# Encoder block in float32: sum transfers paused in the branches, first row block ahead, branch sums on VectorE, temporaries in a pool of their own

## The chip, the cores and the metric

One core of a Trainium2 chip runs the whole program in one launch. The metric is device time in microseconds, from runs of the whole kernel; lower is better. The profile is of one execution on the same core. Engines are named as the profile names them: PE (TensorE), DVE (VectorE), ACT (ScalarE), POOL (GpSimd), SP (SyncE, which only issues transfers here).

## The reference

The input x has 2048 rows of 1024 float32 numbers. One layer is computed, followed by a last RMSNorm:

```
xn = rmsnorm(x);  z = xn @ w_in            # columns: pool | q | forget | input | output gate | branch gates
ya = pool_mixer(z_pool) @ w_pa             # 4 window means minus token, a 128x128 matrix per group
yb = hgrn2(q, forget, input, gate) @ w_pb  # gated linear recurrence, 4 heads of 128
x  = x + (sig(g0) * ya + sig(g1) * yb) @ w_o
h  = rmsnorm(x) @ w_up;  h = conv3(h) + b  # causal, per column
x  = x + (silu(gate half) * value half) @ w_down
return rmsnorm(x)
```

## The kernel before, in words

**Two halves.** The 2048 rows are done in two halves of 1024, and each half is two row blocks of 512 (`hf` 0 and 1). A half runs through the stages io, proj, pa, pb, wo (function `mixer`), then up and dn (`ffn`).

**Products.** Every float32 operand is cut in two parts of the type fp32r, high and low (`split`, L595 to L598: a cast on ACT or POOL, a subtraction on DVE), and a product is three matmuls: high by high, high by low, low by high. A product of a 128x512 operand over four k is 12 matmuls. The large matrix products (io, proj, wo, up, dn) use a Strassen-like scheme with seven products P1 to P7 in place of eight. It needs sums of quarters of the weights (`s1` to `s4`) and of the activations.

**Weights.** `Stream` loads weight tiles on SP's queue into 8 raw buffers (L182), cuts them in two into 6 operand buffers (L205 a cast on ACT, L206 a subtraction on DVE), and hands them out in program order. In the first half the sums of weight quarters for wo, up and dn are made in DRAM by transfers alone, in groups of up to four units (`Sums.make`: copies on ACT's queue, L278, and accumulating transfers on POOL's queue, L275). Each step of a group is a transfer of up to 1 MB. The task `prepare` takes two groups at a time and makes one step every 7 ticks; a tick is counted every 6 matmuls issued through `mm`. In the second half nothing of this runs: the sums are read again.

**The branches.** `pa` multiplies the pooled, mixed rows (`mx`, read back from DRAM by `pa_task` on SP's queue, L796, and split) by w_pa; `pb` does the same for the recurrence's output (`oT`, fetched by the task that `start_o` starts at the loop's step `O_AT`). Each goes over eight column tiles m in the order `M_ORDER` = 0, 4, 1, 5, 2, 6, 3, 7; for each m it makes one product for row block 0 and one for row block 1. The result is multiplied by a gate that is fetched from DRAM (`gl`, L1291 and L1293 on DVE). In pb the two branches are then added on POOL (L1301), and for each k = m - 4 the sums of the scheme are made from four of these tiles (`add_forms`, `yf`, L1090 on POOL).

**The row products.** `Rows` computes wo and dn: the activations' tiles (128x128 blocks of them) are the stationary operand and the weights move. `make(upto)` splits the operands of the steps up to a number; `run(p)` calls it LEAD = 5 steps ahead. At the end of a product, DVE adds PSUM banks to the rows (L1066).

**The up stage.** A `Unit` makes the seven products of one pair of column tiles into three PSUM banks X, Z and V, and takes temporaries e1, u2, u3 (`tmp`, L1018 to L1024). Near the end of up, `EARLY` makes the first operands of dn, whose rows `g_P` are fetched from DRAM on POOL's queue (L796).

**Room.** Most tiles come from one pool, `slots`, of 77 tiles of 128x528 float32. A tile is given out when a former one is released. Instructions are written in program order; the framework plans the order on each engine with a simulated timeline, and adds the waits.

Of the kernel before, what the change touches and what calls it, by code (L numbers as in the profile page):

```python
# [29 lines left out]
TB = 512  # L30
# [16 lines left out]
OUT = R_OUT, R_OUT_BANK, R_OUT_NEW, R_OUT_ADD  # L47
# [7 lines left out]
PROJ = (("fq", 0), ("g", 0), ("u", 0), ("fq", 1), ("g", 1), ("g", 2), ("fq", 2), ("g", 3),  # L55
        ("u", 1), ("g", 4), ("fq", 3), ("g", 5), ("g", 6), ("g", 7))

M_ORDER = (0, 4, 1, 5, 2, 6, 3, 7)

N_SLOTS = 77  # L60
N_RUN = 3
N_HEADS = 2
GO_AT = 5
# [1 line left out]
X_AT, X_AT2 = 1, 4  # L65
GO_IO = (("P2", 1), ("P2", 0))
G_POOL = 4
O_AT, O_LAG = 4, 1
FIN_WAIT = 4
N_RAW = 8  # L70
GROUP = 4
# [7 lines left out]
def tile_trunk(  # L79
# [15 lines left out]
    nc = tc.nc  # L95
    pe, act, dve, pool, sp = nc.tensor, nc.scalar, nc.vector, nc.gpsimd, nc.sync
# [3 lines left out]
    rawp = ctx.enter_context(tc.tile_pool(name="rawp", bufs=N_RAW))  # L100
    opsp = ctx.enter_context(tc.tile_pool(name="opsp", bufs=N_OPS))
    slots = ctx.enter_context(tc.tile_pool(name="slots", bufs=N_SLOTS))
    dram = ctx.enter_context(tc.tile_pool(name="dram", bufs=1, space=bass.MemoryType.DRAM))
    banks = ctx.enter_context(tc.tile_pool(name="banks", bufs=8, space=bass.MemoryType.PSUM))

    def slot(name, cols=TB, dt=F32):
        return slots.tile([P, cols], dt, tag="s", name=name, padded_shape=[P, 528])

    def bank(name, cols=512):
        return banks.tile([P, cols], F32, tag="b", name=name, padded_shape=[P, 512])  # L110
# [33 lines left out]
    def mm(*args, **kw):  # L144
        count[1] = pe.matmul(*args, **kw)  # L145
        count[0] += 1
        if count[0] % MM_PER_TICK == 0:
            tick()
# [102 lines left out]
    stream = Stream()  # L251
# [210 lines left out]
        return grouped(w_up_t, ms, [MF + m for m in ms], list(range(m0, m0 + n)))  # L462

    prep = []

    def prepare():
        todo = [sums[name].make(g) for name in ("wo", "up", "dn")
                for g in range(len(sums[name].groups))]
        active = []
        while todo or active:  # L470
            while todo and len(active) < 2:
                active.append(todo.pop(0))
            g = active.pop(0)
# [320 lines left out]
    def fetch(d, name, eng=sp):  # L794
        t = slot(name)
        eng.dma_start(t, d)  # L796
        return t
# [188 lines left out]
    class Unit:  # L986
# [3 lines left out]
            self.t = {}  # L990

        def tmp(self, k):
            t = slot(f"{self.name}_{k}")
            self.t[k] = t
            return t

# [87 lines left out]
    def add_forms(two, forms, k, name, store=lambda p, t: None, sums=True, pin=lambda i: None):  # L1084

        def comb(p, x0, x1, op):
            if (p, k) in forms or x0 is None or x1 is None:
                return
            t = slot(f"{name}_{p}_{k}")
            pin(pool.tensor_tensor(t, x0, x1, op))  # L1090
# [12 lines left out]
        comb("P3", forms.get(("P6", k)), two.get((1, 1)), ALU.add)  # L1103
# [54 lines left out]
    def mixer(b0, forms, late):  # L1158
# [103 lines left out]
        for n, (kind, i) in enumerate(PROJ):  # L1262
            if (kind, i) == ("u", 0):
                held["w"] = stream.get("pw")
            u = Unit(f"{kind[0]}r{b0}_{i}", "in", emits[kind](i))
            for p in ORDER:
                u.multiply(p, forms, late)
                u.after(p)
                if n == len(PROJ) - 1 and p == "P1":
                    mtask = Task(pa_task())  # L1270

        def branch(key, s, xs, evac, each):
            for n, m in enumerate(M_ORDER):
                each(n)
                for m2 in M_ORDER[n : n + 3]:
                    for hf in range(2):
                        gate(s, m2, hf)
                w4 = stream.get(key)
                for hf in range(2):
                    ps = bank(f"{key}{b0 + hf}_{m}")  # L1280
                    chain_t(ps, lambda k: (w4[:, 0, k * P : (k + 1) * P],
                                           w4[:, 1, k * P : (k + 1) * P]),
                            [xs[hf, k] for k in range(4)])
                    evac(m, hf, gate(s, m, hf), ps)
                stream.used(1)

        y, yf = {}, {}

# [9 lines left out]

        def evac_b(m, hf, g, ps):
            gated(g, hf, g, ps)  # L1300
            pool.tensor_tensor(y[m, hf], y[m, hf], g, ALU.add)  # L1301
# [17 lines left out]
        join(otask[0])  # L1319

        acc = {}

        def load_res(n):
            hf, j = n // NT, n % NT
# [27 lines left out]
    def ffn(b0, forms, late):  # L1352
# [74 lines left out]
        acc = {}  # L1427
        fg = []
        fss = {}
# [6 lines left out]
        def square(hf, j, c):  # L1436
            if (hf, j) not in fss:
                fss[hf, j] = small.tile([P, 4], F32, tag="fss", name=f"fss{b0}_{hf}_{j}")
            act.activation(slot(f"fj{b0}_{hf}_{j}_{c}"), acc[hf, j, c], AF.Square,  # L1439
                           accum_out=fss[hf, j][:, c : c + 1])  # L1440

        def final(hf, j):
            if hf == 1 and not last:
                yield FIN_WAIT
            for c in range(2):
                square(hf, j, c)
            halves = [acc.pop((hf, j, c)) for c in range(2)]
            res = [slot(f"fo{b0}_{hf}_{j}_{c}") for c in range(2)]
            ss = fss[hf, j]
            pool.tensor_tensor(ss[:, 2:3], ss[:, 0:1], ss[:, 1:2], ALU.add)  # L1450
            r = rstd_of(ss[:, 2:3], 1, 1.0 / D, f"f{b0}_{hf}_{j}r")
            yield 3
            rr = (b0 + hf) * TB + j * P
            for c in (1 - hf, hf):
                if (hf, c) == (0, 1):
                    act.activation(res[c], halves[c], AF.Copy, scale=r[:, 0:1])
                    pool.tensor_tensor(res[c], res[c], fg[c], ALU.mult)
                else:
                    dve.scalar_tensor_tensor(res[c], halves[c], r[:, 0:1], fg[c],  # L1459
                                             ALU.mult, ALU.mult)  # L1460
                sp.dma_start(out[rr : rr + P, 512 * c : 512 * c + 512], res[c])

        down = Rows(f"dn{b0}", "dn", DOWN, MF // 2,
                    lambda p, k: fetch(gd[p, k], f"g{b0}_{p}_{k}", pool), acc, 5)
        EARLY = {"P7": 2, "P4": 3}
        units = {}
        for n, (m, p) in enumerate(up_order()):
            if n == GO_AT:
# [7 lines left out]
            drain(1)  # L1476
            if m == MF - 1 and p in EARLY:
                down.make(EARLY[p])

# [61 lines left out]


# [46 lines left out]
```

## Time and profile before

| what | value |
|---|---|
| median of 3 runs | 2625.63 us (2621.32 to 2626.07) |
| profiled execution, first to last instruction (span) | 2614.3 us |
| PE busy in it | 2533.7 us, 97% |
| DVE, ACT, POOL busy | 1967.4, 1168.9, 909.3 us |
| mean granted PE clock | 0.989 |
| HBM read, written | 384.94 MB, 187.17 MB |

The profiled execution's device time is not given apart from its span; the span is 7.0 us below the fastest of the three runs and 11.3 us below their median. Stages are recognised by the tile that PE writes: `io_`, `fr_`/`ur_`/`gr_` (proj), `pa`, `pb`, `wo_P`, `up_`, `dn_P`. In a timeline row stand the start in us, the duration in us, engine, line, operation, output and inputs, shapes and count, and in brackets the idle time of the engine before it and what ended that. An SP row is a transfer being issued.

### The profile page before, as it was taken

How to read it: one execution, taken by the hardware profiler on the slowest of the kernel's cores; microseconds unless marked ns; L12 is line 12 of the kernel's file. 1: busy time of each engine (PE TensorE's matmuls, PEld its weight loads, DVE VectorE, ACT ScalarE, POOL GpSimd, SP SyncE). 2: the span in 40 equal slices, each digit the busy share in tenths (PEclk: the TensorE clock that was granted, in tenths of full speed). 3: DMA queues.
4: the chain of work that ended last, by engine and by line, in shares of the span. 5: the costliest groups of instructions: out<-in, count | busy, mean ns of one | idle time of the engine just before them, and what ended most of it. 6: DMA issues, size and time to landing. Idle time of an engine off the chain costs nothing. (4 is left out here: it accounts for less than half of the span.)

```text
span 2614.3 us, 35569 instructions
## 1 busy us (share of the span) xinstructions
PE 2533.7 (97%) x11464; PEld 2064.8 (79%) x11464; DVE 1967.4 (75%) x3390; ACT 1168.9 (45%) x2204; POOL 909.3 (35%) x1253
## 2 busy tenths in 40 slices
PE   7899999989999999999999999999999999999998
PEld 6788888767778888878878788887787888887887
DVE  7898779358799877876476787774778987787845
ACT  5333434224555544555364344442345554445633
POOL 5544343062444343362141111200623433335402
PEclk9999999999999999999999999999999999999999
DMA  6887868888778897587365344346452445545943
GB/s 221 274 213 211 224 189 242 268 275 214 198 188 241 243 240 198 165 305 255 108 195 157 101 135 121 116 145 218 142 173 84 151 150 148 141 141 185 377 142 105
DMA packets 254059, 496.90 MB, mean 190 GB/s; under 512 B 26736, under 2 KB 43248, under 8 KB 253552
## 3 DMA queue, kind: packets, MB, share of 16 engines
q1 hardware_dynamic: 187968, 319.89, 38.9%
q0 software_dynamic: 41504, 110.64, 16.6%
q10 hardware_dynamic: 24400, 64.08, 7.1%
q8 instruction: 91, 1.49, 0.2%
q14 instruction: 96, 0.79, 0.1%
HBM read 384.94 MB, written 187.17 MB: 219 GB/s over the span
## 5 line engine op out<-in xcount | busy, mean ns | idle before, releaser
L205 ACT CAST ops<-raw 128x512 fp32r<-128x512 f32 x732 | 451.6, 620 | 780.1 <-PE dn_P L145 141.1
L206 DVE TENSOR_TENSOR ops<-raw,ops 128x512 fp32r<-128x512 f32 x732 | 564.1, 775 | 214.2 <-ACT ops L205 208.7
L1381 DVE SCALAR_TENSOR_TENSOR e<-h,cols,e 128x512 f32<-128x512 f32 x176 | 142.4, 813 | 29.9 <-ACT e L1379 26.1
L1379 ACT ACTIVATE e<-h,cols 128x512 f32<-128x512 f32 x176 | 142.6, 814 | 24.2 <-DVE h L984 16.9
L1384 DVE SCALAR_TENSOR_TENSOR e<-h,cols,e 128x512 f32<-128x512 f32 x176 | 133.9, 769 | 3.0
L796 POOL DMA_DIRECT2D g_P<-dg_P x154 | 83.7, 545 | 107.6 <-PE dn_P L145 70.0
L1090 POOL TENSOR_TENSOR gf_P<-e,e 128x512 f32<-128x512 f32 x44 | 67.8, 1542 | 153.1 <-DVE e L1390 97.8
L1090 POOL TENSOR_TENSOR gf_P<-gf_P,e 128x512 f32<-128x512 f32 x44 | 60.1, 1366 | 68.5 <-DVE e L1390 68.1
L1374 POOL COPY h<-h 128x2 f32<-128x2 f32 x88 | 40.7, 482 | 113.9 <-DVE h L982 112.0
L1301 POOL TENSOR_TENSOR ya<-ya,gl 128x512 f32<-128x512 f32 x32 | 45.8, 1460 | 98.4 <-issue 49.1
L1376 POOL COPY hist<-h 128x2 f32<-128x2 f32 x88 | 35.3, 401 | 127.3 <-DVE h L984 125.6
L1234 ACT ACTIVATE gt<-gt,cols 128x512 f32<-128x512 f32 x48 | 34.8, 724 | 90.5 <-DVE gt L984 71.1
L1388 ACT ACTIVATE e<-e 128x512 f32<-128x512 f32 x88 | 55.5, 631 | 37.9 <-DVE e L1384 37.4
L984 DVE TENSOR_TENSOR h<-up_u,up_V 128x512 f32<-128x512 f32 x88 | 60.2, 684 | 15.2 <-PE up_V L145 14.8
L1197 POOL TENSOR_TENSOR q<-q,qs 128x512 f32<-128x512 f32 x16 | 22.5, 1407 | 136.0 <-ACT qs L1196 105.0
L846 POOL COPY qm<-q 128x64 f32<-128x64 f32 x64 | 22.4, 367 | 117.0 <-DVE q L852 21.6
L1066 DVE TENSOR_TENSOR x<-x,wo_P 128x512 f32<-128x512 f32 x88 | 56.4, 690 | 6.2 <-PE wo_P L145 6.1
L1066 DVE TENSOR_TENSOR ac<-ac,dn_P 128x512 f32<-128x512 f32 x72 | 46.6, 683 | 13.4 <-PE dn_P L145 13.3
L1404 POOL DMA_DIRECT2D dg_P<-gf_P x88 | 52.5, 596 | 10.9 <-POOL gf_P L1090 6.5
L1450 POOL TENSOR_TENSOR fss<-fss 128x1 f32<-128x1 f32 x16 | 4.6, 289 | 141.5 <-ACT fj L1439 141.5
L619 POOL TENSOR_SCALAR ro<-so 128x4 f32<-128x4 f32 x16 | 5.2, 323 | 135.6 <-ACT sq L956 135.4
L1018 ACT COPY up_e<-up_X 128x512 f32<-128x512 f32 x44 | 25.8, 586 | 56.7 <-PE up_X L145 51.6
(1265 smaller groups left out, 8332.4 us busy)
## 6 DMA issues: line engine op xcount, KB each, us to landing
g_P<-dg_P POOLq DMA_DIRECT2D x154, 256.0 KB, 6.2
raw<-in_w_up_t SPq DMA_DIRECT2D x132, 256.0 KB, 3.3
raw<-in_w_in_t SPq DMA_DIRECT2D x98, 256.0 KB, 3.3
dg_P<-gf_P POOLq DMA_DIRECT2D x88, 256.0 KB, 3.9
raw<-in_w_io SPq DMA_DIRECT2D x68, 256.0 KB, 4.9
dg_P<-e SPq DMA_DIRECT2D x66, 256.0 KB, 3.3
raw<-in_w_dn SPq DMA_DIRECT2D x66, 256.0 KB, 3.0
x<-in_x SPq DMA_DIRECT2D x64, 256.0 KB, 5.3
```

The lines of the kernel that those rows point to most:

```text
L205: self.mark = act.copy(hi, v)
L206: dve.tensor_tensor(lo, v, f32(hi), ALU.subtract)
L796: eng.dma_start(t, d)
L984: dve.tensor_tensor(dst, t, ps, ALU.add if how == "add" else ALU.subtract)
L1066: dve.tensor_tensor(t, t, ps[j], ALU.add if sg > 0 else ALU.subtract)
L1090: pin(pool.tensor_tensor(t, x0, x1, op))
L1301: pool.tensor_tensor(y[m, hf], y[m, hf], g, ALU.add)
L1379: in_turn(act.activation(t, h[:, 2:], AF.Identity, bias=col(o_cb + mt), scale=col(o_cw + 4 * MF + mt)))
L1381: in_turn(second(dve.scalar_tensor_tensor(t, h[:, 1 : 1 + TB], col(o_cw + 2 * MF + mt), t, ALU.mult, ALU.add)))
L1384: dve.scalar_tensor_tensor(t, h[:, 0:TB], col(o_cw + mt), t, ALU.mult, ALU.add)
L1388: in_turn(act.activation(g, g, AF.Silu))
L1404: pool.dma_start(d, t)
```

## The change

The sum transfers of `prepare` are held from the first product of pa to the last of pb (`paused`). A branch begins with the products of row block 0 for m = 0 and 4 and then does row block 1 for both; from the third m on it goes as before. The fetch of `mx` begins after P4 of the last unit but one of proj, where it began after P1 of the last; that of `oT` begins at step 3 of pa, where it was 4. The sum of the two branches is made by DVE. `Rows` of wo is made ahead of pb, and each k's operand of P1 is split as soon as pb has that k. A `Unit`'s temporaries come from a pool of 8, `slots` has 75 tiles, and the scratch for POOL's transfers is set to 4096 bytes. The final norm's squares are written into the output's tile. `EARLY` makes operands of dn from P6 of the last unit on, and five are made ahead of dn.

```diff
-N_SLOTS = 77
+N_SLOTS = 75
-O_AT, O_LAG = 4, 1
+O_AT, O_LAG = 3, 1
+    tmps = ctx.enter_context(tc.tile_pool(name="tmps", bufs=8))
...
+    paused = [False]
     def prepare():
...
+            while paused[0]:
+                yield 1
             g = active.pop(0)
...
         def tmp(self, k):
-            t = slot(f"{self.name}_{k}")
+            t = tmps.tile([P, TB], F32, tag="t", name=f"{self.name}_{k}", padded_shape=[P, 528])
...
-                if n == len(PROJ) - 1 and p == "P1":
+                if n == len(PROJ) - 2 and p == "P4":
                     mtask = Task(pa_task())
         def branch(key, s, xs, evac, each):
-            for n, m in enumerate(M_ORDER):
-                each(n)
-                for m2 in M_ORDER[n : n + 3]:
-                    for hf in range(2):
-                        gate(s, m2, hf)
-                w4 = stream.get(key)
-                for hf in range(2):
-                    ps = bank(f"{key}{b0 + hf}_{m}")
-                    chain_t(ps, ...)
-                    evac(m, hf, gate(s, m, hf), ps)
-                stream.used(1)
+            ws = {}
+            def product(m, hf):
+                ps = bank(f"{key}{b0 + hf}_{m}")
+                w4 = ws[m]
+                chain_t(ps, ...)
+                evac(m, hf, gate(s, m, hf), ps)
+                if hf:
+                    stream.used(1)
+            order = [(m, 0) for m in M_ORDER[:2]] + [(m, 1) for m in M_ORDER[:2]]
+            order += [(m, hf) for m in M_ORDER[2:] for hf in range(2)]
+            for m, hf in order:
+                n = M_ORDER.index(m)
+                if not hf:
+                    each(n)
+                    for m2 in M_ORDER[n : n + 3]:
+                        for h2 in range(2):
+                            gate(s, m2, h2)
+                    ws[m] = stream.get(key)
+                product(m, hf)
         def evac_b(m, hf, g, ps):
             gated(g, hf, g, ps)
-            pool.tensor_tensor(y[m, hf], y[m, hf], g, ALU.add)
+            dve.tensor_tensor(y[m, hf], y[m, hf], g, ALU.add)
             if m >= KD // 2 and hf:
...
                 add_forms(two, yf, k, f"yf{b0}")
+                wo.make(k + 1)
...
+        paused[0] = True
         branch("pa", 0, mixed, evac_a, start_o)
...
+        wo = Rows(f"wo{b0}", "wo", OUT, KD // 2, lambda p, k: yf[p, k], acc)
...
         branch("pb", 1, oT, evac_b, load_res)
+        paused[0] = False
...
-        wo = Rows(f"wo{b0}", "wo", OUT, KD // 2, lambda p, k: yf[p, k], acc)
...
-            act.activation(slot(f"fj{b0}_{hf}_{j}_{c}"), acc[hf, j, c], AF.Square,
-                           accum_out=fss[hf, j][:, c : c + 1])
+            act.activation(res, acc[hf, j, c], AF.Square, accum_out=fss[hf, j][:, c : c + 1])
...
-        EARLY = {"P7": 2, "P4": 3}
+        EARLY = {"P6": 2, "P7": 3, "P4": 4}
...
-        down.make(3)
+        down.make(5)
...
-    nc = bacc.Bacc("TRN2", target_bir_lowering=False, num_devices=1)
+    nc = bacc.Bacc("TRN2", target_bir_lowering=False, num_devices=1, dynamic_dma_scratch_size=4096)
```

More of the change, by code (lines that the diff above doesn't have):

```diff
@@ L1268, in mixer @@
                 u.after(p)
-                if n == len(PROJ) - 1 and p == "P1":
+                if n == len(PROJ) - 2 and p == "P4":
                     mtask = Task(pa_task())
         def branch(key, s, xs, evac, each):
-            for n, m in enumerate(M_ORDER):
-                each(n)
-                for m2 in M_ORDER[n : n + 3]:
-                    for hf in range(2):
-                        gate(s, m2, hf)
-                w4 = stream.get(key)
-                for hf in range(2):
-                    ps = bank(f"{key}{b0 + hf}_{m}")
-                    chain_t(ps, lambda k: (w4[:, 0, k * P : (k + 1) * P],
-                                           w4[:, 1, k * P : (k + 1) * P]),
-                            [xs[hf, k] for k in range(4)])
-                    evac(m, hf, gate(s, m, hf), ps)
-                stream.used(1)
+            ws = {}
+            def product(m, hf):
+                ps = bank(f"{key}{b0 + hf}_{m}")
+                w4 = ws[m]
+                chain_t(ps, lambda k: (w4[:, 0, k * P : (k + 1) * P],
+                                       w4[:, 1, k * P : (k + 1) * P]),
+                        [xs[hf, k] for k in range(4)])
+                evac(m, hf, gate(s, m, hf), ps)
[12 more added lines that the diff above has]
+                product(m, hf)
         y, yf = {}, {}
@@ L1434, in load_acc, with square @@
                     acc[hf, j, c] = fetch(x2d[b0 + hf, j, c], f"ac{b0}_{hf}_{j}_{c}", pool)
-        def square(hf, j, c):
+        def square(hf, j, c, res):
             if (hf, j) not in fss:
                 fss[hf, j] = small.tile([P, 4], F32, tag="fss", name=f"fss{b0}_{hf}_{j}")
-            act.activation(slot(f"fj{b0}_{hf}_{j}_{c}"), acc[hf, j, c], AF.Square,
-                           accum_out=fss[hf, j][:, c : c + 1])
+            act.activation(res, acc[hf, j, c], AF.Square, accum_out=fss[hf, j][:, c : c + 1])
         def final(hf, j):
@@ L1444, in final @@
                 yield FIN_WAIT
+            res = [slot(f"fo{b0}_{hf}_{j}_{c}") for c in range(2)]
             for c in range(2):
-                square(hf, j, c)
+                square(hf, j, c, res[c])
             halves = [acc.pop((hf, j, c)) for c in range(2)]
-            res = [slot(f"fo{b0}_{hf}_{j}_{c}") for c in range(2)]
             ss = fss[hf, j]
```

## The prediction

> **What bounds the kernel now.** I read the page first (span, busy shares, the chain that ended last), then the sums by stretch for the stages that the change touches, then the waits of TensorE there, then the timeline around each of them.
>
> ```profile
> span 2614.3 us, 35569 instructions
> PE 2533.7 (97%) x11464; PEld 2064.8 (79%) x11464; DVE 1967.4 (75%) x3390; ACT 1168.9 (45%) x2204; POOL 909.3 (35%) x1253
> PE 23%; DVE 1%; ACT 0%; issue 0%; POOL 0%; DVEq 0%; POOLq 0%; ACTq 0%
> 1992.92 5.57 PE up_Z L145 x24
> ```
>
> TensorE is busy 97% of the span, and the chain is almost all TensorE (it could be followed only over the last quarter). The last row, of that chain, gives the pace when nothing is missing: 5.57/24 = 0.232 us per matmul, 2.78 us for a product of 12. So only idle time of TensorE can be won. The next fence has first-half pa, pb, wo and second-half pa, pb, wo, by stretch (us, busy time and instructions of PE, PEld, DVE, ACT, POOL, granted clock, DMA share, GB/s).
>
> ```profile
> 464.50:527.30 62.80, 56.74 (x254) 45.52 (x253) 25.40 (x49) 18.10 (x42) 5.21 (x6) 0.95 0.86 267
> 527.30:579.50 52.20, 46.77 (x193) 36.68 (x191) 26.65 (x35) 8.61 (x15) 32.29 (x25) 0.97 0.88 284
> 579.50:671.00 91.50, 83.95 (x369) 67.39 (x370) 79.61 (x116) 42.00 (x86) 31.70 (x39) 0.98 0.84 229
> 1763.40:1819.30 55.90, 54.20 (x254) 44.31 (x253) 26.25 (x49) 17.79 (x42) 2.41 (x4) 1.00 0.68 215
> 1819.30:1865.20 45.90, 44.67 (x194) 35.92 (x192) 23.21 (x32) 7.25 (x13) 36.15 (x27) 1.00 0.69 231
> 1865.20:1950.20 85.00, 82.06 (x369) 66.23 (x370) 74.13 (x114) 41.83 (x86) 22.39 (x31) 1.00 0.39 124
> ```
>
> The same work takes 6.9, 6.3 and 6.5 us longer in the first half, which alone has the sum transfers: DMA share 0.86 against 0.68, clock 0.95 against 1.00. This is nearly the experiment that pausing them makes.
>
> **Part 1, pause and "first rows lead" (pa and pb, first half).**
>
> ```profile
> 475.42 0.47 ACTq L278 DMA_DIRECT2D su2s<-su2s  x1
> 477.14 1.44 SPq L796 DMA_DIRECT2D mx<-md  x2
> 485.90 0.62 ACT L597 CAST mxs_2h<-mx 128x512 fp32r<-128x512 f32 x1 [7.25 <-DMA mx<-md]
> 486.57 0.80 PE L145 MATMUL pa<-mxs_2h,ops 128*128 128x512 f32 x1 [5.83 <-ACT mxs_2h L597]
> 526.55 0.43 SPq L796 DMA_DIRECT2D oT<-od  x1
> 533.55 0.62 ACT L597 CAST oTs_0h<-oT 128x512 fp32r<-128x512 f32 x1 [5.46 <-DMA oT<-od]
> 534.20 0.69 DVE L598 TENSOR_TENSOR oTs_0l<-oT,oTs_0h 128x512 fp32r<-128x512 f32 x1 [5.39 <-ACT oTs_0h L597]
> 534.22 0.49 PE L145 MATMUL pb<-oTs_0h,ops 128*128 128x512 f32 x1 [4.01 <-ACT oTs_0h L597]
> ```
>
> Both stalls lie in the second product of the branch: the operand of the second row block is not there. The new order puts one more first-block product ahead, so it is wanted 2.78 us later; its fetch task starts two products (pa) or two half-row products (pb) sooner, 5.6 us; 8.3 us together, more than 5.83 or 4.01. Both fetches run on SP's queue, so an early one that must wait for its source holds raw loads behind it; eight raw buffers cover that, and I cost it at nothing. If the cover goes, it costs the rest of that wait. Late next in pa are the gates, fetched behind mx on the same queue: the products run on until the PSUM banks are full. I take 5 of 5.83 in pa and 4 of 4.01 in pb: 9. Bounds: none, and the whole excess over the second half, 6.9 + 6.3 = 13.2 (the slow clock that follows a long stall is in it).
>
> The clock, first as a row: after 4.14 us without work eight matmuls take 3.78 us, and after 1.75 us only 2.13 (second fence).
>
> ```profile
> 1331.59 3.78 PE L145 MATMUL dn_P<-ops,dn_P_10h 128*128 128x512 f32 x8 [4.14 <-ACT dn_P_10h L597]
> ```
>
> ```profile
> 1121.48 2.13 PE L145 MATMUL dn_P<-ops,dn_P_3h 128*128 128x512 f32 x8 [1.75 <-ACT dn_P_3h L597]
> 2399.57 2.12 PE L145 MATMUL dn_P<-ops,dn_P_3h 128*128 128x512 f32 x8 [1.75 <-ACT dn_P_3h L597]
> ```
>
> **What the pause defers.** 32 products of 12 matmuls are 384 matmuls, 64 ticks of six; one sum step comes every 7 ticks, so nine steps move back by 64 x 6 x 0.232 = 89 us in the up stage.
>
> ```profile
> 1006.54 1.21 POOL L275 DMA_DIRECT2D sd2s<-in_w_dn  x1
> 1119.49 0.32 SPq L182 DMA_DIRECT2D raw<-sd1s  x1
> ```
>
> The last step (sd2) then issues near 1096, and sd1, before it in turn, is first read at 1119.5: 20 us to spare. The moved steps lie under the up products, where steps ran before without stalling TensorE. Cost 0; if that margin were gone, a down product would wait for each missing row.
>
> **Part 2, sums on VectorE and earlier row operands (wo, both halves).** First half, then second:
>
> ```profile
> 579.00 4.28 DVE L206 TENSOR_TENSOR ops<-raw,ops 128x512 fp32r<-128x512 f32 x1 [1.04 <-ACT ops L205]
> 579.54 2.13 PE L145 MATMUL wo_P<-ops,wo_P_0h 128*128 128x512 f32 x8 [1.23 <-ACT wo_P_0h L597]
> 585.69 1.77 DVE L598 TENSOR_TENSOR wo_P_1l<-ya,wo_P_1h 128x512 fp32r<-128x512 f32 x1
> 585.83 1.53 PE L145 MATMUL wo_P<-ops,wo_P_0l 128*128 128x512 f32 x4 [4.16 <-DVE wo_P_0l L598]
> 586.87 1.74 POOL L1090 TENSOR_TENSOR yf_P<-yf_P,ya 128x512 f32<-128x512 f32 x1
> 611.63 0.73 PE L145 MATMUL wo_P<-ops,wo_P_0h 128*128 128x512 f32 x2 [2.02 <-DVE x L1066]
> 614.62 0.73 PE L145 MATMUL wo_P<-ops,wo_P_0h 128*128 128x512 f32 x2 [1.33 <-DVE x L1066]
> 1865.16 1.20 PE L145 MATMUL wo_P<-ops,wo_P_0h 128*128 128x512 f32 x4 [1.23 <-ACT wo_P_0h L597]
> 1890.63 0.74 PE L145 MATMUL wo_P<-ops,wo_P_0h 128*128 128x512 f32 x2 [1.61 <-DVE x L1066]
> 1893.62 0.73 PE L145 MATMUL wo_P<-ops,wo_P_0h 128*128 128x512 f32 x2 [1.33 <-DVE x L1066]
> ```
>
> The row product starts late because its first operand is cut in two only behind the branch, and VectorE, asked for the low part, sits in a subtraction of 4.28 us; beside POOL's 1.74 us sums its splits take 1.77 in place of 0.69. Then the third row product waits for bank evacuations on VectorE, which is still behind.
>
> ```profile
> L1301 POOL TENSOR_TENSOR ya<-ya,gl x32: 1263/1300/1762, 544.4 to 1869.9; 128x512 f32<-128x512 f32 x32
> L1293 DVE TENSOR_TENSOR gl<-gl,pb x16: 675/686/690, 543.5 to 1861.2; 128x512 f32<-128x512 f32 x16
> ```
>
> 32 sums leave POOL (32 x 1.30 = 41.6 us) and go to VectorE at 0.69 (22 us, 11 in each pb). There VectorE is busy 26.7 of 52.2 and 23.2 of 45.9 us, so they lie beside TensorE. POOL keeps 16 form sums for each half, and the backlog that ran on past the branch goes. Splits for P1 are issued in the branch, one product sooner. I count all of the start waits, 1.23 + 4.16 + 1.23 = 6.6, and half of the bank waits (2.02 + 1.33 + 1.61 + 1.33 = 6.3), 3.1: 9.7 together. Bounds 0 and 12.9.
>
> The Trainium skill ("SBUF — State Buffer", Who interferes with whom) says that a VectorE instruction with two SBUF inputs and a GpSimd one that reads SBUF exclude each other for a whole instruction. The trace agrees (a split took 0.69 with POOL idle and 1.77 beside its sums), and by that rule the moved sums meet POOL's remaining ones: the lock rival below.
>
> **Part 3, down rows.**
>
> ```profile
> 1120.30 0.63 ACT L1388 ACTIVATE e<-e 128x512 f32<-128x512 f32 x1
> 1120.83 0.60 ACT L597 CAST dn_P_3h<-g_P 128x512 fp32r<-128x512 f32 x1
> ```
>
> The 1.75 us stall before the fourth down row, in both halves, comes from a split that stands behind the last SiLU in ACT's queue. It is now issued at P4 of the last unit, before that work. I take 3 of 3.5; bounds 0 and 3.5. The g fetches on POOL's queue start four products sooner, behind the last sum steps there; a wait on one only brings them back to where they were.
>
> **Part 4, room.** The units' temporaries leave the slot ring (77 to 75) for eight tiles of their own: neutral in proj and up; but in pb two slots fewer, and eight for early splits. The extra tiles are paid for by cutting POOL's DMA scratch to 4096. The final squares write into the output tile: one instruction fewer to give a slot, none fewer to run. All at 0; the trace shows no price for the scratch, and its nearest rows bound it in the rivals.
>
> **Sum.** 9 + 9.7 + 3 = 21.7; 2614.3 - 21.7 = 2592.6. The span stands 11.3 below the median of 2625.63, so 2604. Bounds of the three parts together: 0 and 29.6, 2626 to 2596; with the 4.14 us stall and its slow clock (about 6) gone or doubled by the new order, 2590 to 2632.
>
> **Rivals.**
> *Queue order, not the sums.* SP's fetches stand behind raw loads that wait for a buffer; then pausing does nothing and the stalls only shrink by the later need, 2.78 each, 5.6 in place of 9, and half of part 2 stays. 5.6 + 4.9 + 3 = 13.5: 2612. Against it: the second half has the same queue and 6.3 us less in pb.
> *Lock on VectorE.* Each of the 16 POOL sums of a pb holds up one VectorE instruction by at most 1.30: 23.2 + 11 + 20.8 = 55 us in 45.9. TensorE would wait 9 us there in the second half, and 26.7 + 11 + 20.8 = 58.5, 6 over, in the first: 15 lost of 21.7: 2619. It decides where VectorE passes the stage's length.
> *No gain.* The whole order is planned anew, and three or four stalls like the 4.14 with its slow clock (6.1 each) take the 21.7: 2622 to 2628. For it: such a stall exists, in a place that no part names.
> *Slower: POOL's scratch.*
>
> ```profile
> 1101.65 3.78 POOL L796 DMA_DIRECT2D g_P<-dg_P  x7
> g_P<-dg_P POOLq DMA_DIRECT2D x154, 256.0 KB, 6.2
> ```
>
> Before, seven fetches go out without a wait, each landing in 6.2 us. If the smaller scratch holds only two, a row comes every 3.1 us where a product needs 2.78: 77 x 0.32 = 25 us in each down stage, 2604 + 50 = 2654. It decides below three in flight; with three it is hidden. The Trainium skill ("DMA: Bandwidth & Descriptors", The descriptor swizzle) counts nine 16-byte descriptors on each side per engine for a 1 MiB transfer; as an estimate, 4096 bytes would hold 28 such sets, which speaks against it.
>
> **How the numbers follow.** Forecast 0.50, queue order 0.18, lock 0.12, no gain 0.10, scratch or another slowdown 0.10. The range 2588 to 2622 leaves out half of no gain, the slow case and a little of the forecast's low end, 2 in 10. A change within 0.2% (5.3 us) cannot be told from none. Faster by more is 0.80 (the first three), within 0.10, slower 0.10.
>
> **What would show it.** After: pa and pb of the first half near 56 and 46 us, clock 1.00 and DMA share under 0.75; no sum transfer issued between pa's start and wo's; wo at 85 or less in the first half and 82 in the second; no wait on dn_P_3h; no sum of ya on POOL. Wrong if TensorE waits in pa for gates or banks, if VectorE's two-input instructions in pb average over 1.3 us, if raw loads of sd1 wait for their sums, or if POOL waits before g fetches.

## The result and the profile after

| | median, us | runs |
|---|---|---|
| before | 2624.58 | 2621.32 to 2626.07, 4 runs |
| after | 2583.98 | 2582.21 to 2589.86, 4 runs |
| ratio | 0.9859 | 95% interval 0.9846 to 0.9871 |

The change makes the kernel 1.4% faster. Later the same two kernels ran again: 2584.0 (four runs) against 2620.49 (23 runs), ratio 0.9866 [0.9853, 0.9878], so 36.5 us. The direction was as forecast; the gain of 21.7 was too small and 2604 was 20 us too high. 2584 lies 4 us under the range. One later run of the kernel before took 14184 us and is left out of its ratio.

The first lines of the page after:

```profile
span 2588.1 us, 35623 instructions
PE 2529.4 (98%) x11464; PEld 2062.4 (80%) x11464; DVE 1987.6 (77%) x3422; ACT 1168.2 (45%) x2204; POOL 871.2 (34%) x1221
```

That execution took 2589.86 us, 1.8 more than its span. From here on a second profile of the kernel after (span 2582.0, time 2583.74) stands against a second one of the kernel before (span 2618.1, time 2619.91). The sums by stretch for pa, pb and wo, first the three of the first half before, then first and second half after (columns as in the prediction: us, busy time and count of PE, PEld, DVE, ACT, POOL, granted clock, DMA share, GB/s):

```profile
465.90:530.00 64.10, 57.55 (x253) 45.91 (x252) 26.03 (x50) 18.34 (x42) 5.22 (x6) 0.95 0.87 271
530.00:582.60 52.60, 48.02 (x194) 37.22 (x193) 26.30 (x34) 8.69 (x15) 32.35 (x25) 0.94 0.85 276
582.60:674.00 91.40, 84.13 (x368) 67.76 (x369) 79.52 (x116) 42.05 (x86) 31.62 (x39) 0.96 0.83 227
```

```profile
475.60:529.40 53.80, 53.80 (x252) 44.15 (x252) 29.42 (x57) 18.37 (x43) 2.44 (x4) 1.00 0.70 230
529.40:573.80 44.40, 44.40 (x194) 36.07 (x193) 34.45 (x44) 6.53 (x11) 19.70 (x14) 1.00 0.76 264
573.80:655.10 81.30, 81.30 (x369) 66.22 (x368) 69.16 (x112) 42.24 (x84) 19.80 (x29) 1.00 0.74 222
1739.80:1793.70 53.90, 53.90 (x252) 44.35 (x252) 26.67 (x51) 16.87 (x41) 2.42 (x4) 1.00 0.64 203
1793.70:1838.30 44.60, 44.60 (x194) 36.05 (x193) 34.75 (x44) 6.53 (x11) 18.67 (x14) 1.00 0.70 245
1838.30:1919.80 81.50, 81.50 (x370) 66.27 (x369) 69.11 (x113) 42.21 (x85) 16.36 (x28) 1.00 0.40 130
```

In all six stretches after, PE's busy time equals the stretch, at full clock. Before, in the first half, a part of each was idle (6.55, 4.58, 7.27 us: the length less PE's busy time) and the busy part was itself slower. The table has the length of each stage from its first matmul to the next stage's first, worked out from the start times in the traces, for the kernels that the argument needs; io is left out (82 us in the second half of each). Each column is one execution, and its time lies between 3.5 us under ("dve only") and 7.6 us over ("room") the median of its kernel. The names are explained with the experiments; "pair" is pause and first rows together, "no room, no down" the five branch parts alone.

```
stage      before  pause  first  pause+  pair   dve+   dve    room   no room  no     after
                          rows   order          rows   only          no down  room
proj1      351.5   352.9  355.6  353.0   355.3  353.4  352.9  365.8  353.9    353.7  361.1
pa1         64.1    61.8   65.4   59.7    53.8   64.3   64.0   62.3   53.8     54.6   53.8
pb1         52.5    45.8   54.7   45.8    45.8   51.0   52.4   55.0   44.4     44.4   44.4
wo1         91.5    84.9   90.3   85.0    83.4   83.1   81.6   91.6   81.5     81.5   81.3
up1+dn1    669.1   666.6  666.1  666.2   667.0  665.0  668.3  662.6  666.4    670.1  663.3
proj2      342.3   344.1  343.8  341.2   343.6  342.6  342.2  346.1  340.9    342.7  339.3
pa2+pb2    101.7   101.6  100.0  101.4    99.7  100.2  101.4   92.9   97.9     98.1   98.5
wo2         85.0    84.7   82.7   84.8    82.7   81.5   81.6   85.2   81.3     81.4   81.5
up2+dn2    664.0   667.9  664.6  666.8   667.9  665.5  664.5  664.2   667.5    668.1  662.2
span      2618.1  2608.2 2621.8 2601.5  2597.2 2603.3 2605.9 2624.0 2585.2   2589.8 2582.0
```

(In "room" the second proj ends some matmuls later than elsewhere and pa2 begins with as much less; proj2 and pa2 are read together there.) From before to after pa, pb and wo lose 10.3 + 8.1 + 10.2 in the first half and 3.2 + 3.5 in the second, 35.3 in all. Elsewhere proj of the first half gets 9.6 longer, and up and down of both halves (7.6 together) and proj of the second (3.0) give that back.

### The profile page after: what moved, and what is told of

Same layout as the page of the kernel before. It is cut to its first block, busy times and chain, and to the rows that moved or that the text cites. A ratio compares the mean times of both kernels' runs of the same rounds, so it can differ in the third digit from the quotient of the medians.

```text
span 2588.1 us, 35623 instructions
## 1 busy us (share of the span) xinstructions
PE 2529.4 (98%) x11464; PEld 2062.4 (80%) x11464; DVE 1987.6 (77%) x3422; ACT 1168.2 (45%) x2204; POOL 871.2 (34%) x1221
## 4 chain that ended last, share of the span: by engine, by line
PE 83%; DVE 8%; issue 3%; DMA 3%; POOL 2%; ACT 1%; SPq 0%; DVEq 0%; POOLq 0%; ACTq 0%
PE dn_P L146 14%; PE up_Z L146 13%; PE up_X L146 9%; PE up_V L146 9%; PE wo_P L146 6%; PE gr_Z L146 4%; PE pb L146 3%; PE pa L146 3%; PE gr_X L146 3%; PE gr_V L146 3%; PE fr_Z L146 2%; DVE ops L207 2%; PE pl L863 2%; PE fr_X L146 1%; PE fr_V L146 1%
## 5 line engine op out<-in xcount | busy, mean ns | idle before, releaser
L206 ACT CAST ops<-raw 128x512 fp32r<-128x512 f32 x732 | 451.7, 620 | 784.3 <-PE dn_P L146 148.8
L207 DVE TENSOR_TENSOR ops<-raw,ops 128x512 fp32r<-128x512 f32 x732 | 550.0, 755 | 196.6 <-ACT ops L206 190.4
L1393 POOL COPY hist<-h 128x2 f32<-128x2 f32 x88 | 42.0, 478 | 120.8 <-DVE h L988 115.8
L1094 POOL TENSOR_TENSOR yf_P<-ya,ya 128x512 f32<-128x512 f32 x16 | 21.3, 1334 | 119.0 <-DVE ya L1315 61.2
L863 PE MATMUL pl<-qm,k 128*128 128x192 f32 x256 | 50.6, 343 | 6.4 <-DVE k L919 3.6
L1070 DVE TENSOR_TENSOR ac<-ac,dn_P 128x512 f32<-128x512 f32 x72 | 46.9, 682 | 12.3 <-PE dn_P L146 12.1
L863 PEld LDWEIGHTS pl<-qm,k 128*128 128x128 f32 x256 | 45.5, 200 | 10.3 <-issue 3.4
```

The costliest lines, as they stand in the source:

```text
L206: self.mark = act.copy(hi, v)
L207: dve.tensor_tensor(lo, v, f32(hi), ALU.subtract)
L863: pe.matmul(pa_[:, c * 192 : c * 192 + 192], ks[:, (i + c) * P : (i + c + 1) * P], mv[:, c].rearrange("p s x -> p (s x)"), start=True, sto ...
L1070: dve.tensor_tensor(t, t, ps[j], ALU.add if sg > 0 else ALU.subtract)
```

## The experiments

Each median is of five rounds, beside runs of the kernel before in the same group: 2620.41 (21 runs), 2620.49 (23), 2620.95 (11) and 2619.67 (7). So the level of the kernel before is near 2620.4; its first three runs, with a median of 2625.63, were high.

**The kernel before again**, unchanged.

> The kernel before, unchanged, for a second profile. Its first profile has a span of 2614.3 us while its timed runs have a median of 2624.6; the changed kernel's profiled execution lies only 1.7 us above its span. Theory L (level): the first profile was a quick execution, about 9 us below a usual one, so the forecast's sum was set on a level that does not hold; the spans here lie mostly between 2618 and 2625, and the extra time stands in the first half's proj, pa, pb or wo, where the sum transfers run. Rival: the span is typical and some 10 us lie around it in every run; then spans stay near 2614 and times near 2625.

2621.13, ratio 1.0001 [0.9992, 1.0010]. Its span is 2618.1, where the first profile had 2614.3: the first profiled execution was a quick one, and one profile of a kernel is not its level. Its waits of PE from pa to wo in the first half (engine, tile and line, what it waited for: us in all, times, longest):

```profile
PE pa L145 <- ACT mxs_2h L597: 6.3, 2, 5.2
PE wo_P L145 <- DVE wo_P_0l L598: 4.2, 1, 4.2
PE wo_P L145 <- DVE x L1066: 3.0, 2, 1.7
PE pb L145 <- ACT oTs_0h L597: 2.0, 1, 2.0
PE wo_P L145 <- ACT wo_P_0h L597: 1.2, 1, 1.2
```

**The pause alone.**

```diff
+            while paused[0]:
+                yield 1
...
+        paused[0] = True          # ahead of branch("pa", ...)
...
+        paused[0] = False         # behind branch("pb", ...)
```

> The kernel before with the pause of the sum transfers alone. Theory S (starts; the transfers cause the late operands): 8 to 13 us faster, first-half pa near 56 and pb near 46 us, DMA share there under 0.75, the 5.83 and 4.01 us waits gone or under 2. Rival Q (order on SP's queue): under 3 us, both waits still above 3. Rival R (room is what counts): under 3 us as well, but with the waits gone and given back elsewhere.

2606.93, ratio 0.9950 [0.9938, 0.9963], 13.5 us. pa keeps most of its excess, pb loses 6.7 and wo 6.6. Waits from the same list, and the sums by stretch for pa and pb:

```profile
PE wo_P L145 <- DVE x L1069: 1.8, 2, 1.3
...
PE wo_P L145 <- DVE wo_P_0l L601: 0.8, 1, 0.8
```

```profile
468.20:530.10 61.90, 58.19 (x254) 45.98 (x253) 28.11 (x53) 19.20 (x44) 2.83 (x4) 0.94 0.63 206
530.10:575.80 45.70, 44.51 (x193) 35.83 (x191) 26.30 (x32) 7.18 (x13) 36.38 (x27) 1.00 0.73 255
```

The stall in pb is gone and that for wo's low part is 0.8 in place of 4.2, with no sum moved to another engine. The transfers show why: between pa's and wo's start the fetches of `oT` and `mx` and a load of weights for pb (`raw`) took this long from issue to landing (median, last column), before and with the pause.

```profile
oT<-od SPq DMA_DIRECT2D x8, 256.0 KB, 5.7
...
mx<-md SPq DMA_DIRECT2D x5, 256.0 KB, 4.4
raw<-in_w_pb_t SPq DMA_DIRECT2D x5, 256.0 KB, 6.2
```

```profile
oT<-od SPq DMA_DIRECT2D x8, 256.0 KB, 4.0
mx<-md SPq DMA_DIRECT2D x5, 256.0 KB, 4.1
raw<-in_w_pb_t SPq DMA_DIRECT2D x5, 256.0 KB, 3.0
```

So it was the sums' traffic that made `oT` and the weights of pb late. `mx` lands hardly sooner: pa's waits for its splits fall from 6.5 to 2.0 us in all, but 3.7 us of pa are still idle and its clock stays at 0.94. The rival "queue order, not the sums", by which pausing does nothing, falls.

**First rows lead, alone**: the new order of products and both earlier fetches.

```diff
-O_AT, O_LAG = 4, 1
+O_AT, O_LAG = 3, 1
-                if n == len(PROJ) - 1 and p == "P1":
+                if n == len(PROJ) - 2 and p == "P4":
+            order = [(m, 0) for m in M_ORDER[:2]] + [(m, 1) for m in M_ORDER[:2]]
+            order += [(m, hf) for m in M_ORDER[2:] for hf in range(2)]
```

> The kernel before with the new order of a branch and the earlier fetch tasks alone; the sum transfers run on. Theory S: 3 to 9 us faster, the waits in pa and pb of the first half shrink by 5 or more together, DMA share in pa and pb stays at 0.86. Rival Q: about 5 to 6 us, each wait smaller by 2.8. If pausing alone is worth as much, the two overlap.

2617.61, ratio 0.9992 [0.9983, 1.0001]: nothing that can be told. The waits of PE:

```profile
PE wo_P L145 <- DVE wo_P_0l L598: 6.2, 1, 6.2
PE pb L145 <- DVE ya L1301: 5.1, 1, 5.1
PE pa L145 <- DVE ya L1301: 5.0, 1, 5.0
PE pb L145 <- DVE ya L1303: 2.7, 1, 2.7
```

No product waits for `mxs` or `oTs` any more; instead they wait for PSUM banks, which VectorE empties with the gate multiplications (L1301, L1303 here). The rows ahead of the two longest waits show what held VectorE:

```profile
525.75 0.62 ACT L597 CAST oTs_2h<-oT 128x512 fp32r<-128x512 f32 x1 [7.16 <-DMA oT<-od]
526.40 0.69 DVE L598 TENSOR_TENSOR oTs_2l<-oT,oTs_2h 128x512 fp32r<-128x512 f32 x1 [6.41 <-ACT oTs_2h L597]
528.36 0.68 DVE L1301 SCALAR_TENSOR_TENSOR ya<-gl,pa 128x512 f32<-128x512 f32 x1
529.10 0.79 PE L145 MATMUL pa<-mxs_0h,ops 128*128 128x512 f32 x1 [5.00 <-DVE ya L1301]
544.78 0.69 DVE L598 TENSOR_TENSOR oTs_2l<-oT,oTs_2h 128x512 fp32r<-128x512 f32 x1 [7.79 <-ACT oTs_2h L597]
546.80 0.80 PE L145 MATMUL pb<-oTs_0h,ops 128*128 128x512 f32 x1 [5.09 <-DVE ya L1301]
```

It is not the gates: VectorE sits in front of a split of `oT` that has not landed, and the gate multiplications stand behind that split in its order. So the late `oT` now stalls TensorE by way of the banks.

**Pause and first rows together**, both edits above.

> The pause, the new order of a branch and the earlier fetch tasks together. With the new order alone, TensorE waited 5.0 and 5.1 us for products' banks whose gates were late; with the pause alone pa kept its length. Theory I (each removes what the other leaves): pa of the first half falls to 54 to 56 us and pb to 45 to 46, no wait on a bank there, 20 to 24 us faster than before in all (13 from the pause, 2 alone from the order, some 7 from the pair). Rival: the parts only add, about 15 us, and pa's fall to 54 in the changed kernel came from the freed room; then pa stays above 60.

2595.69, ratio 0.9907 [0.9892, 0.9921], 24.8 us, where one alone gives 13.5 and the other nothing. PE's waits, and the stretches of pa, pb and wo:

```profile
PE wo_P L145 <- DVE x L1069: 1.3, 2, 0.7
PE wo_P L145 <- ACT wo_P_0h L600: 1.2, 1, 1.2
```

```profile
471.10:525.00 53.90, 53.90 (x254) 44.33 (x253) 29.46 (x56) 19.07 (x44) 2.45 (x4) 1.00 0.71 228
525.00:570.70 45.70, 44.52 (x193) 35.83 (x191) 19.64 (x28) 6.12 (x11) 38.45 (x29) 1.00 0.74 256
570.70:654.20 83.50, 82.13 (x369) 66.19 (x370) 72.15 (x113) 42.13 (x85) 22.76 (x30) 1.00 0.73 215
```

**Pause and order, with the fetches as late as before**: the pair without the two lines on `O_AT` and `PROJ`.

> The pause and the new order of products, with the fetch tasks started as late as before. Theory O (the later need is enough once transfers are quick): within 2 us of 2595.7, pa 54 to 56. Rival T (the earlier fetch is what counts): a wait of 2 us or more for mxs or oTs stays in pa or pb, 2600 or more.

2605.55, ratio 0.9943 [0.9930, 0.9957], 15.4 us. Against the pair the earlier fetches are worth 9 us. The order by itself adds some 2 to the pause, which the overlapping intervals do not tell from nothing. The fetches with the pause and without the order were not run. pa still waits 1.3 us for its rows (`mxs_2h`).

**Sums on VectorE and earlier row operands.**

```diff
-            pool.tensor_tensor(y[m, hf], y[m, hf], g, ALU.add)
+            dve.tensor_tensor(y[m, hf], y[m, hf], g, ALU.add)
+                wo.make(k + 1)            # and wo = Rows(...) ahead of pb
```

> The kernel before with the branch sums on VectorE and the row operands split inside pb, nothing else. Theory S: 8 to 13 us faster; no wait of TensorE at wo's start in either half (1.23, 4.16, 1.23 before), bank waits (2.02, 1.33, 1.61, 1.33) half or less. Rival lock: pb longer than 52.2 and 45.9 us by 6 or more and VectorE's two-input instructions there above 1.3 us; then same or slower.

2603.6, ratio 0.9936 [0.9923, 0.9950], 16.8 us: wo loses 8.4 and 3.5 in the two halves, pb 1.5 and 1.3.

**The sums on VectorE alone**, the first two lines of that diff.

> The branch sums on VectorE alone, row operands split behind pb as before. Theory V (POOL's backlog delayed VectorE's splits): about 12 us faster, the 4.2 us wait for wo_P_0l and most bank waits gone, the 1.23 at each start of wo left. Rival W (the early splits are what counts): 5 us or less, with bank waits of 2 and 1.3 still there.

2611.13, ratio 0.9963 [0.9951, 0.9976], 9.8 us; by the medians the earlier row operands add 7, of which the table shows only 2.6 in the spans, since this profiled execution was the fastest of its five. pb is as long as before here (52.4 of 52.5), so what pb gained above came with them. PE's waits in wo here:

```profile
PE wo_P L145 <- ACT wo_P_0h L597: 1.2, 1, 1.2
```

The low part `wo_P_0l` and the banks (`x`) are gone from the list. The weight subtractions of DVE in 30 us from about wo's start show why (count, busy us, mean ns), before and with the sums on VectorE:

```profile
L206 DVE TENSOR_TENSOR ops<-raw,ops 128x512 fp32r<-128x512 f32 x4 | 6.4, 1602 | 0.9 <-ACT ops L205 0.9
```

```profile
L206 DVE TENSOR_TENSOR ops<-raw,ops 128x512 fp32r<-128x512 f32 x7 | 5.3, 770 | 0.0
```

POOL's sums end 3 us behind wo's start where they ended 16 us behind it, and a subtraction (L206) takes 770 ns there in place of 1602.

**Room alone**: the pool of temporaries, 75 slots, the scratch and the final squares.

```diff
-N_SLOTS = 77
+N_SLOTS = 75
+    tmps = ctx.enter_context(tc.tile_pool(name="tmps", bufs=8))
-            t = slot(f"{self.name}_{k}")
+            t = tmps.tile([P, TB], F32, tag="t", ...)
-            act.activation(slot(f"fj..."), acc[hf, j, c], AF.Square, ...)
+            act.activation(res, acc[hf, j, c], AF.Square, ...)
+    nc = bacc.Bacc(..., dynamic_dma_scratch_size=4096)
```

> The room alone: temporaries in a pool of 8, slots 75, scratch 4096, squares into the output tile. Theory N (neutral, as forecast): within 3 us either way, no wait of POOL before its transfers, the time of a 256 KB issue on POOL near 0.55 us. Rival R (ring relief counts): 5 us or more faster, with proj or up shorter. Rival C (scratch): slower, POOL's issues longer and the down stages longer.

2618.54, ratio 1.0000 [0.9991, 1.0010]. Its profiled execution (2626.12 us) was its slowest, 7.6 over the median, so the stages are not exact. But they show that the nothing is a sum of parts: the first proj gets 14.3 longer (9.6 to 12.3 in the other profiles of kernels with the pool), up and down of both halves 6.3 shorter, the second proj with pa 4.9 shorter. The sums by stretch of the operations on the tile `q` in 112 to 480 us, here and then for the kernel before:

```profile
112.00:480.00 368.00, 31.92 (x242) 28.71 (x242) 52.91 (x128) 22.41 (x64) 24.47 (x40) 0.99 0.77 217
```

```profile
112.00:480.00 368.00, 33.60 (x252) 30.17 (x253) 45.50 (x128) 21.98 (x64) 21.93 (x40) 1.00 0.79 224
```

And the recurrence's groups of PE that wait for DVE there, in the same order (count, busy us, mean ns, idle before it and for what; with the room the second of them waits 1.1):

```profile
L860 PE MATMUL pl<-qm,k 128*128 128x192 f32 x128 | 26.3, 350 | 6.6 <-DVE k L916 3.6 <-DVE qm L851 3.0
```

```profile
L859 PE MATMUL pl<-qm,k 128*128 128x192 f32 x128 | 22.8, 326 | 0.0
L895 PE MATMUL pl<-q,k 128*128 128x128 f32 x128 | 16.8, 277 | 2.8 <-DVE q L820 2.8
```

The 128 DVE operations on `q` take 52.91 us in place of 45.50, and these matmuls of the recurrence wait 7.7 us for DVE where they waited 2.8. Why the operations take longer is not shown. The scratch shows no price. The g fetches on POOL (count, busy us, mean ns of an issue) are

```profile
L797 POOL DMA_DIRECT2D g_P<-dg_P x154 | 83.3, 542 | 112.8 <-PE dn_P L146 79.1 <-DMA g_P<-dg_P 11.2 <-issue 4.8
```

and they land 5.8 us after their issue; before, an issue took 545 ns and a landing 6.2 us.

**Down rows alone.**

```diff
-        EARLY = {"P7": 2, "P4": 3}
+        EARLY = {"P6": 2, "P7": 3, "P4": 4}
-        down.make(3)
+        down.make(5)
```

> The earlier operands of dn alone. In the changed kernel the wait before the fourth down row is gone and one before the fifth has come, 2.60 us in the first half and 1.23 with 0.98 in the second. Theory M (the wait moves one row on): within 2 us of before, with such waits on dn_P_4 here as well. Rival (as forecast): 3 us faster, and the moved wait belongs to another part of the change.

2618.49, ratio 1.0001 [0.9992, 1.0010]. A row of PE's timeline in the first half:

```profile
1128.20 2.12 PE L145 MATMUL dn_P<-ops,dn_P_4h 128*128 128x512 f32 x8 [1.57 <-ACT dn_P_4h L597]
```

The wait on `dn_P_3h` (1.75 in both halves) is now one on `dn_P_4h`, 1.57 here and 1.23 in the second half.

**The changed kernel again.**

> The changed kernel, unchanged, for a second profile. Its first profile is of the slowest of its four runs (span 2588.1, the others 2580.5 to 2583.5) and has 363.7 us in proj of the first half where before has 351.7. Theory X (that execution): proj of the first half comes out between 352 and 358 and the span between 2579 and 2585. Rival P (the new plan): 362 or more again, in every execution, and the rest of the stages shorter by what the span is shorter. About 37 us faster than before in either case.

2584.0, ratio 0.9866 [0.9853, 0.9878], as the first time.

**The five branch parts**: pause, order, fetches, sums on VectorE, row operands; no room, no down rows.

> Pause, new order, fetch tasks, VectorE sums and row operands together, without the room and without the earlier dn operands: a candidate for a better version, since proj of the first half is 10 us longer with the room. Theory A (the branch parts carry everything, the room moves work between stages): 2588 to 2591, from the pair's 2595.7 less about 7 (wo 2 and 1, pb 1.4 and 1.3, dn 1), proj of the first half back at 352 to 355, proj of the second 343. Rival B (the room only costs): 2574 to 2580, proj at 352 and all else as in the changed kernel.

2588.36, ratio 0.9879 [0.9866, 0.9891], 32.6 us. The pair and the VectorE parts would add to 24.8 + 16.8 = 41.6; together they give 9 less. In wo of the first half they remove the same start: 8.1 and 8.4 alone, 10.0 together, 6.5 of overlap.

**The changed kernel less the room**, and **less the down rows**.

> The changed kernel without the room (77 slots, temporaries among them, default scratch, squares into tiles of their own). Theory A: 2587 to 2591, as without the earlier dn operands, so that the room is worth 4 to 6 us in this company though nothing alone. Rival D (the dn operands carry that): 2582 to 2585. Rival B: 2580 or less.

> The changed kernel without the earlier dn operands: a candidate for the best version. Theory: the earlier operands only move a wait one row on and cost 4 us in the kernel without the room (2592.7 against 2588.4), so here 2579 to 2582. Rival: with the room they cost nothing, 2583 to 2586.

2592.66, ratio 0.9892 [0.9880, 0.9905], and 2587.88, ratio 0.9876 [0.9861, 0.9891]. So without the room the changed kernel is some 8.7 slower, though the room by itself is worth nothing. Without the down rows it is 4 slower, with overlapping intervals. By the medians the room is worth something only beside the early down operands: without them it is 2587.88 against 2588.36. Up and down of the first half take 670.1 with those operands and no room, and 663.3 with both (666.4 with neither, 663.7 with the room alone).

**The five branch parts with one part of the room**: with the final squares only, and with the pool, slots and scratch only.

> Pause, order, fetch tasks, VectorE sums and row operands, and of the room only the squares written into the output tile; no earlier dn operands. Theory Q (the squares' 32 tiles hold back the tail of the down stage): 2583 to 2586, the down stage of the first half 2 to 4 us shorter than 226.8, proj of the first half still 354. Rival P (the pool of temporaries is what helps): 2587 to 2590, nothing changed.

> The same five parts with the pool of temporaries, 75 slots and the small scratch, squares as before; no earlier dn operands. Theory Q: 2588 or more, proj of the first half near 361 and proj and up of the second 2 to 4 us shorter, which is a wash. Rival P: 2580 to 2584, the whole worth of the room.

2585.3, ratio 0.9864 [0.9846, 0.9882], and 2589.41, ratio 0.9879 [0.9862, 0.9895]. The first cannot be told from the changed kernel, and does without the pool and the down rows. The stages separate the two parts. With the squares alone proj of the first half takes 354.4 us, as without the room (353.9), and its down stage up to the second half's io takes 223.8 in place of 226.8. With the pool, slots and scratch alone proj takes 362.0 and the down stage 227.5. So the longer first proj comes with the pool and its slots, and the shorter first down stage with the squares. No version tried was clearly faster than the changed kernel.

## Why the prediction was right and wrong, step by step

**The step that failed is the size of Part 1.** Taken one after the other, the measured gains are 24.8 us for Part 1 (9 counted), 7.8 more with Part 2 (9.7 counted) and 3.9 more with Parts 3 and 4 (3 and 0 counted): 36.5 in place of 21.7. Part 1 alone is 15.8 over. That the other parts nearly came out is luck: measured alone, Part 2 is 16.8 and Parts 3 and 4 are nothing.

**The level: wrong, 5 us.** The sum was made against a span of 2614.3, and then 11.3 us were added, by which that span stood below the median. What lies around a span is 1.8 us. The rest was that the profiled execution was a quick one (2614.3 + 1.8 = 2616.1, near the lowest of the later runs, 2615.32) and that the three runs shown were high (2625.63 against 2620.4 later). Of the 20 us by which 2604 missed, 5.2 are this (2625.6 - 2620.4); the other 14.8 are the size of the gain, 36.5 in place of 21.7.

**Part 1, 9 us: the mechanism held, the size failed.** The pair measured 24.8. Three things were left out of the step.
First the clock. The forecast counted the wait ahead of one instruction (5 of 5.83, 4 of 4.01) and kept the slow clock behind it for the bound. The stretches show what it was worth: from before to the pair pa's busy time fell from 57.55 to 53.90, pb's from 48.02 to 44.52, wo's from 84.13 to 82.13, together 9.2 of the 25.0 us that these three lost, while the clock rose to 1.00 from values of 0.94 to 0.96. In the second half of the kernel before, at a clock of 1.00, the same work was busy for 54.20, 44.67 and 82.06. The Trainium skill ("TensorE: Matmul & The Clock Gate", Part 1) has the throttled clock as the default that sustained activity releases; by that rule a removed stall pays twice, and the trace agrees with these rows.
Second, the start of wo: the pair alone took 8.1 from it, all of which the prediction had booked under Part 2. With the pause alone the wait for `wo_P_0l` is 0.8 where it was 4.2. POOL's sums then end 9 us behind wo's start and not 16, so VectorE has less of them beside it there; that this is the reason is likely but was not tested.
Third, the bound. "The whole excess over the second half", 13.2, was no upper end, since pa and pb of the second half were themselves not free of stalls: they shrank by 3.2 too.

The "late next" was named wrongly. With the order but without the pause, PE does wait in pa and pb for banks, 12.8 us in three waits, and nothing is gained. But ahead of the two longest (10.1 us) VectorE stood waiting for `oT`, not for gates. The earlier fetch was costed at nothing; while the sum transfers run, what it fetches lands late (`oT` 7.4 us from issue to landing, 5.7 before) and holds up the emptying of banks behind it. So the new order and the fetches need the pause, which the forecast did not say. With the pause, the fetches are worth 9 us, and the order can hardly be told from nothing.

**What the pause defers, 0: held.** Issues of the sum transfers after (start, duration, engine), and the first load of `sd1s`:

```profile
449.37 1.70 POOL L276 DMA_DIRECT2D su2s<-in_w_up_t  x1
...
578.25 1.22 POOL L276 DMA_DIRECT2D su1s<-in_w_up_t  x1
...
1082.79 1.20 POOL L276 DMA_DIRECT2D sd2s<-in_w_dn  x1
```

```profile
1104.96 0.32 SPq L183 DMA_DIRECT2D raw<-sd1s  x1
```

No sum transfer of POOL goes out between those two, from before pa's first product to behind pb's last; one copy on ACT's queue (`su1s`) goes out at 568.5, 5 us before pb ends. The last step issues 76 us later than before, at 1083 where 1096 was expected, 22 us ahead of the first load of `sd1s`; what PE waits for in down is splits of rows, below, not these loads.

**Part 2, 9.7 us: held in kind, too small in size.** Alone it measured 16.8. The bank waits were counted by half; with the sums on VectorE they are gone entirely. So wo lost 11.9 where 9.7 was counted, and pb lost 2.8, which was costed at nothing and came with the earlier row operands; the other 2 us lie in stages that the edit doesn't touch. In the company of Part 1 it adds 7.8 (from 24.8 to 32.6), since the start of wo can be mended only once.

**Lock on VectorE (2619): did not decide.** The sums do meet POOL's. The sums of the two branches over the whole trace after (min/median/max ns), and in pb of the first half (busy, mean ns):

```profile
L1315 DVE TENSOR_TENSOR ya<-ya,gl x32: 676/688/1794, 533.8 to 1840.3; 128x512 f32<-128x512 f32 x32
```

```profile
L1315 DVE TENSOR_TENSOR ya<-ya,gl 128x512 f32<-128x512 f32 x15 | 13.4, 895 | 0.2
```

A sum takes up to 1794 ns there, 895 on average. The exclusion that the Trainium skill states ("SBUF — State Buffer", Who interferes with whom) thus agrees with the rows, but costs 3.1 us over fifteen sums where the rival had 20.8, and VectorE is busy 34.45 of 44.40 us. Below its point of decision it costs TensorE nothing.

**Part 3, 3 us: failed.** The split was late not only because of its place in the queue: made sooner, the wait passes to the next row. Alone it measured 0; the changed kernel still has it:

```profile
1107.34 2.11 PE L146 MATMUL dn_P<-ops,dn_P_4h 128*128 128x512 f32 x8 [1.57 <-ACT dn_P_4h L601]
1312.27 2.81 PE L146 MATMUL dn_P<-ops,dn_P_10h 128*128 128x512 f32 x8 [2.83 <-ACT dn_P_10h L601]
2370.17 2.14 PE L146 MATMUL dn_P<-ops,dn_P_4h 128*128 128x512 f32 x8 [1.23 <-ACT dn_P_4h L601]
```

The prediction asked what is late next for pa and did not ask it here. The stall before `dn_P_10h` (4.14 and 3.93 before) has shrunk to 2.83, which no part had forecast. It comes with the squares of Part 4: 2.54 to 3.10 us in the five profiles of kernels that have them, 3.47 to 4.20 in the twelve of kernels that have not.

**Part 4, 0: right as measured alone, wrong in company.** The forecast took "neutral in proj and up" as no effect; it is a loss of about 10 to 14 us in the first proj, which comes with the pool and its slots, against gains in up, down and the second proj. The squares were put at nothing ("one instruction fewer to give a slot"), and go with 3 us less in the first down stage. Why the room pays only beside the early down operands stays open: that they take slots which the units' temporaries would need is likely, but no experiment separated it.

**The signs named for the profile.** pa and pb of the first half came to 53.8 and 44.4 (56 and 46 named), the clock to 1.00, wo to 81.3 and 81.5; no wait on `dn_P_3h` is left. The DMA share is 0.70 in pa but 0.76 in pb, over the 0.75 named, and costs nothing there.

**POOL's scratch (2654): fell.** With the room alone an issue takes 542 ns and a landing 5.8 us; in the changed kernel they take 541 ns and 6.4 us, where before has 545 and 6.2. **No gain (2622 to 2628): fell**, though its mechanism, a new order with new stalls, is what happened in the first proj.

## What to carry to other kernels

Cost a stall with the slow clock behind it and with the work it delays in the next stage: here the slow clock was 9 of the 25 us that three stages lost. When an operand arrives late beside heavy transfers, ask what stands behind it in the order of the engine that takes it: asked for sooner but still late, `oT` held up the emptying of banks. Taking the traffic away, fetching sooner and wanting it later gave 25 us together, while the last two without the first gave nothing. Two edits that remove the same start wait are not added. And a bundle that measures nothing can hide a loss and a gain: its parts are worth a run each.

## What the runs showed of the hardware

Beside sum transfers of up to 1 MB, loads of 256 KB on another queue took 5.7 us (`oT`) and 6.2 us (weights of pb) from issue to landing, and 4.0 and 3.0 without; `mx` was hardly slowed, 4.4 and 4.1. A subtraction on VectorE (L206) took 1602 ns on average where GpSimd was busy 17.35 of 30 us with its sums, and 770 where it was busy 5.12. The same kernel's profiled executions differed by 3.8 us in span before (2614.3 and 2618.1) and by 6.1 after (2588.1 and 2582.0), so that one profile cannot carry a level to better than that.
